# Halving by tokens at both ends of every stage, and moving the memory projections forward, in a two-layer decoder trunk

## The chip, the cores and the metric

One core of a Trainium2 chip runs the whole program. The metric is the device time of one execution in microseconds (us). TensorE (PE) does the matrix products, VectorE (DVE), ScalarE (ACT) and GpSimd (POOL) the rest; SyncE (SP) issues nearly all transfers.

## What is computed

Two layers, each of four sub-layers with the same frame: a norm before, a norm of the result, and the sum with the residual x (512 tokens, 1024 features).

```
for l in range(DEPTH):
    y = swiglu(rms_norm(x, ffn1_pre_g[l]), ...)              # 1024 -> 2816 -> 1024
    x = x + 0.5 * rms_norm(y, ffn1_post_g[l])
    y = hybrid_mixer(rms_norm(x, mix_pre_g[l]), ...)         # windowed attention heads and retention heads
    x = x + rms_norm(y, mix_post_g[l])
    y = memory_xattn(rms_norm(x, xa_pre_g[l]), rms_norm(mem, xa_mem_g[l]), wq[l], wk[l], wv[l], wo[l])
    x = x + rms_norm(y, xa_post_g[l])
    y = swiglu(rms_norm(x, ffn2_pre_g[l]), ...)
    x = x + 0.5 * rms_norm(y, ffn2_post_g[l])
```

The keys and values of the 256 memory tokens (wk, wv) depend on the memory alone, not on x.

## The kernel before

Everything is float32, in feature-major tiles: x is 8 chunks of 128 features by 512 tokens. Each operand of a product is split into a high part (rounded to the fast float32 format) and the remainder, and `mm3` (L113) adds three matmuls: high by high, high by low, low by high.

**Weights** come as units of 128 x 1024 (512 KB). `unit` (L79) fetches one over SP's queue into one of 3 raw buffers, ACT writes the high part (L85) and DVE the low part (L86) into one of 4 buffer pairs. A unit is 8 chunks k of 128 x 128, so 24 matmuls over 512 tokens.

**A stage's end.** The output projection (`out_proj` L215, or the last group of `ffn` L291) makes the 8 chunks of y; each chunk's squares are added to ssq. `postnorm` (L205) transposes ssq on PE (L162), sums it (L164), takes an inverse root by Newton steps of 11 tiny DVE operations (L129), and transposes that back to rows (L173). Then for each chunk: yn (DVE, L211), the sum into x (POOL, the first on DVE, L212), and the next stage's operand: xsh (ACT, L183) and xsl (DVE, L184).

**A stage's beginning.** The norm before a stage commutes with the product, so products start from xsh and xsl while `prenorm` (L189) squares x, sums, transposes and makes the row of scales `rstd_bc`. Results are scaled as they leave PSUM. There are 4 PSUM buffers for products (`acc`) and 4 for other work (`aux`), so 4 units can be done before `rstd_bc` is there.

**Fillers.** A stage is handed the memory work as `filler`: `mem_keys` (L369, 24 matmuls of 256 columns a unit) and `mem_values` (L381) stand ahead of the stage's own products, and `mem_split` (L356), which makes the memory's operand in 8 slots of the tag "xs", is `prep` of the stage before, six times in all. The tag "xs" has 16 slots, which also hold xsh and xsl.

**Halves already.** Before the last ffn there is no memory work left. There `out_halves` (L230) does the last two chunks of the projection by halves of 256 tokens, with `postnorm` of each half right behind it, and the first two units of the ffn run by halves too (L268).

**Order.** The text is not the order on the engines. The Tile library lists each engine's instructions ahead of time: the text's order is the priority, and what it expects to be ready later stands later. Each engine then runs its list strictly in order. So fillers and products mix matmul by matmul, and a wait that lasts longer than the list expected holds up all that stands behind it.

Of the kernel before, what the change touches and what calls it, by code (L numbers as in the profile page):

```python
# [17 lines left out]
P = 128  # L18
# [7 lines left out]
GROUPS = ((0, 8), (8, 15), (15, 22))  # L26
HALVES = (slice(0, T // 2), slice(T // 2, T))
# [20 lines left out]
def trunk(ctx: ExitStack, tc: tile.TileContext, a: dict, out: bass.AP):  # L48
# [9 lines left out]
    slots = {"b": 24, "xs": 16, "h": 16, "kv": 6}  # L58
# [34 lines left out]


    nc.sync.dma_start(small[0], a["small"][0])
    nc.sync.dma_start(x[0], a["xT"][0])
    first = {0: unit(a["ffn1_gu"][0, 0, 0], 1024)}
    for c in range(1, 4):
        nc.sync.dma_start(x[c], a["xT"][c])
    first[1] = unit(a["ffn1_gu"][0, 0, 1], 1024)  # L100
# [44 lines left out]
    def sumsq(acc_t, src, c, eng):  # L145

        if c == 0:
            n = src.shape[-1]
            acc_t = big("ssq")[:, :n]
            act.activation(acc_t, src, AF.Square)  # L150
            return acc_t
# [37 lines left out]
    def prenorm():  # L189
# [3 lines left out]
        ssq, part = None, None  # L193
        for c in range(4):
            ssq = sumsq(ssq, x[c], c, pool)
        for c in range(4, NC):
            part = sumsq(part, x[c], c - 4, dve)
        dve.tensor_tensor(ssq, ssq, part, op=ALU.add)
        cols = rms_cols(ssq, D, T)
        ps = row_bc(cols, NT)  # L200
        bc = big("rstd_bc")
        act.activation(bc, ps, AF.Copy)
        return xh, xl, cols, bc

    def postnorm(y, ssq, gains, nxt, ts_=slice(0, T)):  # L205

        w = ts_.stop - ts_.start
        ps = row_bc(rms_cols(ssq[:, ts_], D, w), w // P)
        for c in range(NC):
# [3 lines left out]
            split_x(c, nxt, ts_)  # L213

    def out_proj(src, l, oh, ol):  # L215

        y, ssq = [], None
        for c in range(NC):
            wh, wl = unit(src[l, c], 1024)
            ps = acc("ps_o")  # L220
            for k in range(NC):
                s = slice(k * P, (k + 1) * P)
                mm3(ps, wh[:, s], wl[:, s], oh[k], ol[k], k == 0, k == NC - 1)
            ssq = sumsq(ssq, ps, c, dve if c == NC - 1 else pool)
            yc = big("y")
            dve.tensor_copy(yc, ps)
            y.append(yc)
        return y, ssq

    def out_halves(src, l, oh, ol, gains, nxt):  # L230

        y, ssq, w = [], None, {}
        for c in range(NC):
            wh, wl = unit(src[l, c], 1024)
            y.append(big("y"))
            if c >= NC - 2:
                w[c] = wh, wl
                continue
            ps = acc("ps_o")
            for k in range(NC):  # L240
                s = slice(k * P, (k + 1) * P)
# [15 lines left out]
    def ffn(l, which, gains, nxt, filler=None, prep=None, halves=False):  # L257
        gu, dn = FF_UNITS[which]
        if filler:
            filler()  # L260
# [682 lines left out]
```

## Time and profile before

| | |
|---|---|
| median of 3 runs | 2509.0 us (2507.91 to 2514.05) |
| the profiled execution's own time | 2508.29 us |
| its span, first to last instruction | 2506.5 us |
| busy share PE, DVE, ACT, POOL | 97%, 56%, 36%, 10% |
| HBM traffic | 229.53 MB read, 92 GB/s over the span |
| mean granted TensorE clock | 0.995 |

Busy time of PE is modelled: a 512-column matmul is shown with 0.39 us while the next one starts 0.227 us after it, so the first 0.16 us of a wait look busy. Read the starts, not the bars.

### The profile page before, as it was taken

To read this page: it belongs to the slowest core of one execution; us is meant where nothing else is said; L and a number is where in the kernel's file an instruction comes from. 1 tells how busy PE (TensorE), PEld (TensorE's weight loads), DVE (VectorE), ACT (ScalarE), POOL (GpSimd) and SP (SyncE) were. 2 spreads that over 40 slices of the span, in tenths; PEclk is the share of its full clock that TensorE was granted. 3 is DMA by queue.
4 is the path that set the end of the run, shared out by engine and by line. 5 is a ranking of instruction groups with operands and counts; after the bars stand their busy time and mean duration, and the time that the engine had idled before them with its cause. 6 is when DMAs were issued, how large, how long until landed. Compare 5 with 4: busy or idle time off the path is not lost. (4 is left out here: it accounts for less than half of the span.)

```text
span 2506.5 us, 30782 instructions
## 1 busy us (share of the span) xinstructions
PE 2431.5 (97%) x12052; PEld 2020.5 (81%) x12052; DVE 1400.2 (56%) x2536; ACT 902.4 (36%) x1480; POOL 258.8 (10%) x218
## 2 busy tenths in 40 slices
PE   8999999999999999999999999999999998999997
PEld 6888878888877878888878888868888777888887
DVE  6434458465776484344484344584657766634454
ACT  4322243255344443222343222332553443322222
POOL 0000022001040120000120000130010402100002
PEclk9999999999999999999999999999999999999999
DMA  4333333411232233233333333324112222232321
GB/s 173 98 100 94 99 121 108 143 45 34 76 109 84 93 101 93 101 93 100 110 98 96 101 93 101 106 89 150 44 35 70 93 76 68 86 100 92 102 90 62
DMA packets 74593, 233.62 MB, mean 93 GB/s; under 512 B 8272, under 2 KB 17744, under 8 KB 74448
## 3 DMA queue, kind: packets, MB, share of 16 engines
q1 hardware_dynamic: 65232, 222.21, 27.9%
q10 hardware_dynamic: 9216, 9.44, 1.2%
q8 instruction: 95, 1.56, 0.3%
q14 instruction: 50, 0.41, 0.1%
HBM read 229.53 MB, written 2.10 MB: 92 GB/s over the span
## 5 line engine op out<-in xcount | busy, mean ns | idle before, releaser
L85 ACT ACTIVATE whi<-raw 128x1024 fp32r<-128x1024 f32 (+2 forms) x402 | 417.8, 1041 | 1097.6 <-PE ps_gu L115 324.0
L86 DVE TENSOR_TENSOR wlo<-raw,whi 128x1024 fp32r<-128x1024 f32 (+2 forms) x402 | 491.2, 1223 | 292.7 <-ACT whi L85 284.4
L114 PE MATMUL ps_gu<-xsh,whi 128*128 128x512 f32 (+1 forms) x1424 | 552.3, 389 | 13.8 <-ACT whi L85 9.3
L115 PE MATMUL ps_gu<-xsl,whi 128*128 128x512 f32 (+1 forms) x1424 | 555.0, 390 | 9.9 <-DVE xsl L184 9.7
L116 PE MATMUL ps_gu<-xsh,wlo 128*128 128x512 f32 (+1 forms) x1424 | 552.8, 388 | 0.0
L115 PEld LDWEIGHTS ps_gu<-xsl,whi 128*128 128x128 f32 x1424 | 268.6, 189 | 71.2 <-DVE xsl L184 17.7
L114 PEld LDWEIGHTS ps_gu<-xsh,whi 128*128 128x128 f32 x1424 | 269.0, 189 | 69.2 <-ACT whi L85 9.2
L116 PEld LDWEIGHTS ps_gu<-xsh,wlo 128*128 128x128 f32 x1424 | 268.8, 189 | 55.4 <-DVE wlo L86 1.8
L154 POOL TENSOR_TENSOR ssq<-ssq,sq 128x512 f32<-128x512 f32 (+1 forms) x84 | 131.4, 1564 | 1708.7 <-ACT sq L153 1705.6
L115 PE MATMUL ps_dn<-hl,whi 128*128 128x512 f32 (+1 forms) x704 | 268.5, 382 | 2.4 <-DVE hl L123 2.4
L114 PE MATMUL ps_dn<-hh,whi 128*128 128x512 f32 (+1 forms) x704 | 268.2, 381 | 0.0
L116 PE MATMUL ps_dn<-hh,wlo 128*128 128x512 f32 (+1 forms) x704 | 268.0, 381 | 0.0
L278 DVE TENSOR_TENSOR u<-ps_gu,rstd_bc 128x512 f32<-128x512 f32 x88 | 60.8, 691 | 215.4 <-PE ps_gu L116 215.3
L274 DVE TENSOR_TENSOR g<-ps_gu,rstd_bc 128x512 f32<-128x512 f32 x88 | 60.8, 691 | 183.9 <-PE ps_gu L116 179.4
L115 PEld LDWEIGHTS ps_dn<-hl,whi 128*128 128x128 f32 x704 | 132.3, 188 | 28.9 <-DVE hl L123 3.8
L114 PEld LDWEIGHTS ps_dn<-hh,whi 128*128 128x128 f32 x704 | 132.4, 188 | 26.2 <-ACT hh L122 0.5
L116 PEld LDWEIGHTS ps_dn<-hh,wlo 128*128 128x128 f32 x704 | 132.4, 188 | 25.1
L301 DVE TENSOR_TENSOR y<-ps_dn,y 128x512 f32<-128x512 f32 x56 | 38.7, 691 | 132.3 <-PE ps_dn L116 132.3
L115 PE MATMUL ps_fm<-xsl,whi 128*128 128x512 f32 x256 | 103.2, 404 | 4.0 <-DVE xsl L184 3.8
L114 PE MATMUL ps_fm<-xsh,whi 128*128 128x512 f32 x256 | 103.0, 404 | 0.0
L116 PE MATMUL ps_fm<-xsh,wlo 128*128 128x512 f32 x256 | 101.3, 396 | 0.6 <-DVE wlo L86 0.6
L612 ACT ACTIVATE p<-p,smx 128x512 f32<-128x512 f32 (+3 forms) x128 | 70.5, 552 | 87.2 <-DVE smx L610 87.0
(226 smaller groups left out, 3723.0 us busy)
## 6 DMA issues: line engine op xcount, KB each, us to landing
raw<-in_ffn_gu_dram SPq DMA_DIRECT2D x176, 512.0 KB, 3.3
raw<-in_ffn_dn_dram SPq DMA_DIRECT2D x64, 448.0 KB, 3.3
raw<-in_ffn_dn_dram SPq DMA_DIRECT2D x32, 512.0 KB, 3.5
raw<-in_win_fm_dram SPq DMA_DIRECT2D x32, 512.0 KB, 3.3
raw<-in_wk_dram SPq DMA_DIRECT2D x16, 512.0 KB, 3.5
raw<-in_cmp_w_dram SPq DMA_DIRECT2D x16, 512.0 KB, 3.7
raw<-in_wout_dram SPq DMA_DIRECT2D x16, 512.0 KB, 3.5
raw<-in_wv_dram SPq DMA_DIRECT2D x16, 512.0 KB, 3.5
```

The costliest lines, as they stand in the source:

```text
L85: act.activation(hi, raw, AF.Copy)
L86: dve.tensor_tensor(lo, raw, hi.bitcast(F32), op=ALU.subtract)
L114: pe.matmul(ps, ah, bh, start=start, stop=False)
L115: pe.matmul(ps, ah, bl, start=False, stop=False)
L116: pe.matmul(ps, al, bh, start=False, stop=stop)
L154: eng.tensor_tensor(acc_t, acc_t, sq, op=ALU.add)
L274: dve.tensor_tensor(g1, pss[0], bc, op=ALU.mult)
L278: dve.tensor_tensor(u1, pss[1], bc, op=ALU.mult)
L301: dve.tensor_tensor(y[c], ps, y[c], op=ALU.add)
L612: act.activation(pr[i], pr[i], AF.Exp, bias=m, scale=-1.0, accum_out=sums[:, i : i + 1])
```

## The change

Six things:

1. **Tail.** Every stage but the last ends with `project`: chunks 0 to 5 as before, then chunks 6 and 7 by halves of tokens from weights that `tail_unit` splits into 8 slots of "xs". Both halves' sums and rows come ahead of both `postnorm`s in the text.
2. **Lead.** `lead` starts every stage but the first with three units, fetched early, chunk by chunk: for the first 256 tokens and k = 0 to 7 all three units take their turn, then for the other 256. Three more whole units follow, two of them in `aux` buffers, before any result needs `rstd_bc`.
3. **Squares.** The squares of x are taken in each half's `postnorm` (`add_squares`), no longer in the next stage.
4. **Memory work.** Keys and values of layer 0 (16 units) stand in the first ffn's last group, ahead of chunk 5; layer 1's keys (8) in the ffn behind it and its values (8) in the third ffn. `mem_split` runs three times. No stage has a filler.
5. **Queries.** Cross-attention makes six of its eight query units in `lead`; only the last head's two are left among the heads.
6. **Buffers.** "b" has 23 slots for 24, "kv" 8 for 6, and memory chunks are fetched through 2 buffers for 3.

```diff
+FM_LEAD = (6, 7, 0, 1, 2, 3)
+N_LEAD, N_MORE, N_TAIL = 3, 3, 2
...
-    slots = {"b": 24, "xs": 16, "h": 16, "kv": 6}
+    slots = {"b": 23, "xs": 16, "h": 16, "kv": 8}
...
+    early = {}
+    def fetch(key, src):
+        early[key] = unit(src, 1024)
+    def unit_of(key, src):
+        return early.pop(key) if key in early else unit(src, 1024)
+    def tail_unit(src, n):
+        raw = raw_unit(src, n)
+        parts = []
+        for k0 in range(0, n, 512):
+            m = min(512, n - k0)
+            h_, l_ = big("dh", F32R, tag="xs")[:, :m], big("dl", F32R, tag="xs")[:, :m]
+            act.activation(h_, raw[:, k0 : k0 + m], AF.Copy)
+            dve.tensor_tensor(l_, raw[:, k0 : k0 + m], h_.bitcast(F32), op=ALU.subtract)
+            parts += [(h_[:, k : k + P], l_[:, k : k + P]) for k in range(0, m, P)]
+        return parts
...
+    squares = []
+    def add_squares(ts_):
+        if not squares:
+            squares.extend([big("ssq"), big("ssq")])
+        ssq, part = squares
+        for c in range(NC):
+            to, eng = (ssq, pool) if c < 4 else (part, dve)
+            sumsq(None if c % 4 == 0 else to[:, ts_], x[c][:, ts_], c % 4, eng, to[:, ts_])
+        dve.tensor_tensor(ssq[:, ts_], ssq[:, ts_], part[:, ts_], op=ALU.add)
+    def lead(keys, srcs, name, halves=True):
+        n = N_LEAD if halves else 2
+        units = [unit_of(key, src) for key, src in zip(keys[:n], srcs)]
+        pss = [acc(name) for _ in units]
+        for ts_ in HALVES if halves else (slice(0, T),):
+            for k in range(NC):
+                s = slice(k * P, (k + 1) * P)
+                for (wh, wl), ps in zip(units, pss):
+                    mm3(ps[:, ts_], wh[:, s], wl[:, s], xh[k][:, ts_], xl[k][:, ts_], k == 0, k == NC - 1)
+        ssq, part = squares
+        squares.clear()
+        act.activation(bc, row_bc(cols, NT), AF.Copy)
+        for i in range(n, len(keys)):
+            wh, wl = unit_of(keys[i], srcs[i])
+            ps = acc(name) if i < 4 else aux(name)
+            for k in range(NC):
+                s = slice(k * P, (k + 1) * P)
+                mm3(ps, wh[:, s], wl[:, s], xh[k], xl[k], k == 0, k == NC - 1)
+            pss.append(ps)
+        return xh, xl, pss, cols, bc
...
+        add_squares(ts_)
+    def project(src, n, oh, ol, y, ssq, gains, nxt, get=None, at=None):
+        first_y, w = y[0] is None, {}
         for c in range(NC):
+            if c == NC - N_TAIL - 1 and at:
+                at()
+            if c >= NC - N_TAIL:
+                w[c] = tail_unit(src(c), n * P)
+                if first_y:
+                    y[c] = big("y")
+                continue
+            wh, wl = unit(src(c), n * P)
             ps = acc("ps_o")
+            for k in range(n):
                 s = slice(k * P, (k + 1) * P)
+                mm3(ps, wh[:, s], wl[:, s], oh[k], ol[k], k == 0, k == n - 1)
+            if first_y:
+                y[c] = big("y")
+                dve.tensor_copy(y[c], ps)
+            else:
+                dve.tensor_tensor(y[c], ps, y[c], op=ALU.add)
+            ssq = sumsq(ssq, ps if first_y else y[c], c, pool)
+        if get:
+            get()
+        rows = []
         for ts_ in HALVES:
             for c in w:
                 ps = acc("ps_o")[:, : T // 2]
+                for k in range(n):
+                    mm3(ps, w[c][k][0], w[c][k][1], oh[k][:, ts_], ol[k][:, ts_], k == 0, k == n - 1)
+                yc = y[c][:, ts_]
+                if first_y:
+                    dve.tensor_copy(yc, ps)
+                else:
+                    dve.tensor_tensor(yc, ps, yc, op=ALU.add)
                 sq = big("sq")[:, : T // 2]
+                act.activation(sq, ps if first_y else yc, AF.Square)
                 dve.tensor_tensor(ssq[:, ts_], ssq[:, ts_], sq, op=ALU.add)
+            rows.append(row_bc(rms_cols(ssq[:, ts_], D, T // 2), NT // 2))
+        for ts_, ps in zip(HALVES, rows):
+            postnorm(y, ps, gains, nxt, ts_)
...
+    def fetch_ffn(l, which):
+        for i in range(N_LEAD):
+            f, b = divmod(i, 2)
+            fetch((which, l, f, b), a[FF_UNITS[which][0]][l, f, b])
...
+            if last:
+                project(lambda c: a[dn][l, c][:, f0 * P : f1 * P], n, hh, hl, y, None, gains, nxt, get, at)
+                return
...
-            m = bp.tile([P, MEM], F32, name="memc", tag="mc", bufs=3)
+            m = bp.tile([P, MEM], F32, name="memc", tag="mc", bufs=2)
...
-        for h in range(4):
-            if h > 0 or l == 0:
-                split_kv(h)
...
+        ready = [query(c) for c in range(n)]
+        for h in range(4):
+            if h > 0:
+                split_kv(h)
+            qs = [split(ready.pop(0) if ready else query(c), "xq") for c in range(2 * h, 2 * h + 2)]
...
-    ffn(0, "ffn1", half1[0], gcols(0, G_MIXPRE), prep=first_prep)
-    mixer(0, gcols(0, G_XAPRE), filler=keys(0, 0, 7), prep=split_mem(0))
-    xattn(0, gcols(0, G_F2PRE), filler=lambda: (mem_keys(0, 7, 8), mem_values(0, 0)), mid=values(0, 1), prep=split_mem(1))
-    ffn(0, "ffn2", half2[0], gcols(1, G_F1PRE), filler=keys(1, 0, 4), prep=split_mem(1))
-    ffn(1, "ffn1", half1[1], gcols(1, G_MIXPRE), filler=keys(1, 4, 8), prep=split_mem(1))
-    mixer(1, gcols(1, G_XAPRE), filler=values(1, 0), prep=split_mem(1))
-    xattn(1, gcols(1, G_F2PRE), filler=values(1, 1), halves=True)
-    ffn(1, "ffn2", half2[1], None, halves=True)
+    add_squares(slice(0, T))
+    ffn(0, "ffn1", half1[0], gcols(0, G_MIXPRE), get=lambda: fetch_fm(0), prep=both(mem_norm, split_mem(0)),
+        at=both(keys(0, 0, 8), values(0, 0), values(0, 1)), halves=False)
+    mixer(0, gcols(0, G_XAPRE), get=lambda: fetch_wq(0))
+    xattn(0, gcols(0, G_F2PRE), get=lambda: fetch_ffn(0, "ffn2"))
+    ffn(0, "ffn2", half2[0], gcols(1, G_F1PRE), get=lambda: fetch_ffn(1, "ffn1"), prep=split_mem(1),
+        at=both(keys(1, 0, 8)))
+    ffn(1, "ffn1", half1[1], gcols(1, G_MIXPRE), get=lambda: fetch_fm(1), prep=split_mem(1),
+        at=both(values(1, 0), values(1, 1)))
+    mixer(1, gcols(1, G_XAPRE), get=lambda: fetch_wq(1))
+    xattn(1, gcols(1, G_F2PRE), get=lambda: fetch_ffn(1, "ffn2"))
+    ffn(1, "ffn2", half2[1], None)
```

## Rows read from the trace of the kernel before

**Rows 1.** Page, part 1: busy us (share of the span) xinstructions.

```profile
PE 2431.5 (97%) x12052; PEld 2020.5 (81%) x12052; DVE 1400.2 (56%) x2536; ACT 902.4 (36%) x1480; POOL 258.8 (10%) x218
```

**Rows 2.** Busy time of PE by windows, one for each stage change: window, length, busy (xmatmuls), clock, DMA share, GB/s.

```profile
372.00:425.00 53.00, 47.53 (x294) 0.97 0.30 96
722.00:772.00 50.00, 43.70 (x194) 0.97 0.29 95
865.00:930.00 65.00, 60.88 (x309) 1.00 0.30 98
1230.00:1300.00 70.00, 64.70 (x328) 1.00 0.33 106
1620.00:1680.00 60.00, 55.16 (x238) 1.00 0.28 89
1970.00:2025.00 55.00, 49.80 (x227) 1.00 0.30 96
2085.00:2160.00 75.00, 66.30 (x370) 0.95 0.26 83
```

**Rows 3.** The same windows for tile ps_mk alone (PE, weight loads, DVE).

```profile
372.00:425.00 53.00, 22.53 (x168) 21.78 (x168) 2.65 (x7) 0.97 0.30 96
865.00:930.00 65.00, 12.13 (x96) 11.76 (x96) 1.66 (x4) 1.00 0.30 98
```

**Rows 4.** Timeline of PE: start, duration, line, tiles; 512 columns, then 256.

```profile
54.82 0.39 PE L115 MATMUL ps_gu<-xsl,whi 128*128 128x512 f32 x1
55.05 0.39 PE L116 MATMUL ps_gu<-xsh,wlo 128*128 128x512 f32 x1
...
2107.15 0.28 PE L115 MATMUL ps_o<-xol,whi 128*128 128x256 f32 x1
2107.27 0.28 PE L116 MATMUL ps_o<-xoh,wlo 128*128 128x256 f32 x1
```

**Rows 5.** Timeline of the change that already goes by halves, [idle before <-releaser].

```profile
2107.59 0.38 ACT L252 ACTIVATE sq<-ps_o 128x256 f32<-128x256 f32 x1 [2.50 <-PE ps_o L116]
...
2111.96 0.41 PE L173 MATMUL bc_ps<-cst,rs_y 128*128 128x128 f32 x2 [0.35 <-DVE rs_y L141]
...
2115.93 0.50 PE L114 MATMUL ps_gu<-xsh,whi 128*128 128x256 f32 x2 [1.43 <-ACT xsh L183]
...
2126.40 0.43 PE L173 MATMUL bc_ps<-cst,rs_y 128*128 128x128 f32 x2 [2.78 <-DVE rs_y L141]
...
2129.65 0.58 PE L114 MATMUL ps_gu<-xsh,whi 128*128 128x256 f32 x1 [2.82 <-ACT xsh L183]
```

**Rows 6.** Timeline of DVE: first yn and last xsl of that change's second half.

```profile
2126.87 0.87 DVE L211 SCALAR_TENSOR_TENSOR yn<-y,small,bc_ps 128x256 f32<-128x256 f32 x2 [0.53 <-PE bc_ps L173]
...
2135.69 0.49 DVE L184 SCALAR_TENSOR_TENSOR xsl<-x,small,xsh 128x256 fp32r<-128x256 f32 x1 [0.29 <-ACT xsh L183]
```

**Rows 7.** Groups by line and form: xcount | busy us, mean ns | idle before.

```profile
L184 DVE SCALAR_TENSOR_TENSOR xsl<-x,small,xsh 128x512 fp32r<-128x512 f32 x56 | 63.6, 1136 | 6.6 <-PE ps_mv L116 3.4 <-ACT xsh L183 3.1
L184 DVE SCALAR_TENSOR_TENSOR xsl<-x,small,xsh 128x256 fp32r<-128x256 f32 x16 | 8.5, 549 | 1.8 <-ACT xsh L183 1.8
L154 DVE TENSOR_TENSOR ssq<-ssq,sq 128x256 f32<-128x256 f32 x2 | 0.9, 426 | 1.1 <-ACT sq L153 1.1
L212 POOL TENSOR_TENSOR x<-x,yn 128x256 f32<-128x256 f32 x14 | 11.5, 849 | 18.6 <-DVE yn L211 18.6
```

**Rows 8.** Windows: ps_tm at the end of the first mixer's heads, and all engines (PE, loads, DVE, ACT, POOL) in the second cross-attention.

```profile
640.00:656.00 16.00, 15.47 (x67) 12.50 (x67) 2.44 (x4) 1.00 0.44 142
...
2016.00:2083.00 67.00, 66.47 (x341) 52.83 (x339) 41.34 (x82) 30.29 (x67) 0.00 (x0) 1.00 0.13 43
```

**Rows 9.** Windows, all engines, behind the longest wait of the kernel.

```profile
2124.00:2136.00 12.00, 6.78 (x31) 6.34 (x32) 9.71 (x30) 4.65 (x10) 5.75 (x7) 0.72 0.14 44
```

**Rows 10.** Page part 6 (KB each, us to landing) and DVE's weight split of part 5.

```profile
raw<-in_wk_dram SPq DMA_DIRECT2D x16, 512.0 KB, 3.5
L86 DVE TENSOR_TENSOR wlo<-raw,whi 128x1024 fp32r<-128x1024 f32 (+2 forms) x402 | 491.2, 1223 | 292.7 <-ACT whi L85 284.4
```

More of the change, by code (lines that the diff above doesn't have):

```diff
@@ L265, in ffn @@
             for f in range(f0, f1):
-                w = [first.pop(b) if b in first else unit(a[gu][l, f, b], 1024) for b in range(2)]
-                pss = [acc("ps_gu") for _ in range(2)]
-                for ts_ in HALVES if halves and f == 0 else (slice(0, T),):
-                    for (wh, wl), ps in zip(w, pss):
-                        for k in range(NC):
-                            s = slice(k * P, (k + 1) * P)
-                            mm3(ps[:, ts_], wh[:, s], wl[:, s], xh[k][:, ts_], xl[k][:, ts_], k == 0, k == NC - 1)
+                pss = []
+                for b in range(2):
+                    if lead_ps:
+                        pss.append(lead_ps.pop(0))
+                        continue
+                    wh, wl = unit(a[gu][l, f, b], 1024)
+                    ps = acc("ps_gu")
+                    for k in range(NC):
+                        s = slice(k * P, (k + 1) * P)
+                        mm3(ps, wh[:, s], wl[:, s], xh[k], xl[k], k == 0, k == NC - 1)
+                    pss.append(ps)
                 g1 = big("g1")
@@ L301, in ffn @@
                     dve.tensor_tensor(y[c], ps, y[c], op=ALU.add)
-                if last:
-                    ssq = sumsq(ssq, y[c], c, dve if c == NC - 1 else pool)
-        postnorm(y, ssq, gains, nxt)
     def down_halves(src, f0, n, hh, hl, y, gains):
@@ L358, in mem_split @@
         for c in range(NC):
[L359 removed]
+            m = bp.tile([P, MEM], F32, name="memc", tag="mc", bufs=2)
             nc.scalar.dma_start(m, a["memT"][c])
@@ L395, in mem_values, with mixer @@
             kv["v", l, m, half] = t
-    def mixer(l, nxt, filler=None, prep=None):
+    def mixer(l, nxt, get=None, prep=None, at=None):
         sm = small[l]
-        if filler:
-            filler()
-        xh, xl, cols, bc = prenorm()
+        xh, xl, lead_ps, cols, bc = lead([("fm", l, j) for j in FM_LEAD], [a["win_fm"][l, j] for j in FM_LEAD], "ps_fm")
+        lead_ps = dict(zip(FM_LEAD, lead_ps))
         def fm(j):
+            if j in lead_ps:
+                return lead_ps.pop(j)
             wh, wl = unit(a["win_fm"][l, j], 1024)
@@ L758, in split_kv, with query @@
                     vv[m, h // 2] = pair(kv["v", l, m, h // 2], "xv")
[L760 to L770 removed]
+        split_kv(0)
+        n = N_LEAD + N_MORE
+        xh, xl, lead_ps, cols, bc = lead([("wq", l, c) for c in range(n)], [a["wq"][l, c] for c in range(n)], "ps_xq")
+        oh, ol = [], []
+        def query(c):
+            if lead_ps:
+                ps = lead_ps.pop(0)
+            else:
                 wh, wl = unit(a["wq"][l, c], 1024)
```

102 lines of the change are left out of this document (25 added, 77 removed).

## The prediction

> **What bounds the kernel now.** The page first: PE is busy 97% of the span, no other engine over 56%, PE's weight loads aside [rows 1]. The kernel is its matmuls, so a change can only cut their number, their spacing, or PE's waits. Nothing here cuts the number. Spacing comes next, from the timeline: in a stream of 512-column matmuls one starts 0.227 us after another, of 256 columns 0.120 [rows 4]. Two halves cost 0.240, so halving adds 0.013 us a matmul and 0.040 a chunk of three.
>
> Then the waits, by windows around the seven stage changes [rows 2]. They hold 428 us and, less a dozen that began earlier, 1948 matmuls. Of these 600 have 256 columns (384 are memory keys, of which 168 and 96 stand in [rows 3]; the window at 722 has 24 and that at 1230 again 96; 192 are halves in the last window, 24 are scores), 126 are narrow at 0.11 (16 transposes a window), and 1222 have 512. At their spacings that is 72 + 14 + 277 = 363 us; **65 us are lost**, about 9 a change, although 90 us of memory work (384 key matmuls, 46 us, and 192 value matmuls of 512 columns, 44) ran in and around six of them. Part of it is the clock: behind a wait from 2123 to 2130 [rows 5] the granted clock averages 0.72 over 12 us [rows 9], that is, part of the time at 1.2 instead of 2.4 GHz, 3.4 us lost. The windows at 372 and 722 show 0.97, 1.6 us each.
>
> The last window matters most: it has no memory work and already goes by halves, and it loses 14 us, the most of all. There the second half's scales reached PE after a wait of 2.78 us and its first operand after 2.82 more [rows 5], because the text put the first half's `postnorm` ahead of the second half's sums.
>
> **The change part by part.** The sum is made against the profiled execution, 2508.3 us, which lies 0.7 under the median.
>
> *Halves, on PE's path.* A lead has 3 units x 8 chunks x 0.040 = 0.96 us more, a tail 2 x 8 x 0.040 = 0.64 (7 chunks in an ffn: 0.56). Seven leads, four tails of 8 and three of 7 make 6.7 + 2.6 + 1.7 = 11.0. The last change pays 1.3 of this already: **+9.7 us**.
>
> The Trainium skill, "TensorE: Matmul & The Clock Gate", section "Back-to-back issue gap", gives 518 cycles for 512 columns and 262 for 256, so two halves would cost 6 cycles or 2.5 ns more, and the whole term 2 us. Here rows 4 show 13 ns; the row decides.
>
> *What is lost at a change afterwards.* Count from the end E of the first half's tail. The first yn can start 4.8 us later: from the square at 2107.59 to the end of the row transposes at 2112.37 [rows 5]. PE meanwhile has the second half's tail, 48 x 0.120 = 5.8 us. The next stage's first matmul needs yn, sum and xsh besides, some 1.5 us, plus 0.4 in an ffn, where y is summed before it is squared: PE waits about 1.0. In the trace it was 1.43 [rows 5].
>
> DVE sets the rest. One half of `postnorm` with DVE nearly to itself took 9.3 us, from the first yn at 2126.87 to the end of the last xsl at 2136.18 [rows 6]. Two are 18.6. Between them, by the order of the text, stand the second half's last sums and its Newton steps (at most 3.6: the first half's chain of 4.8 less ACT's square of 0.38 and two lots of transposes of 0.41) and the first half's squares, 4 x 0.43 = 1.7 [rows 7]. Without overlap the last xsl ends at E + 4.8 + 18.6 + 5.3 = E + 28.7 and PE's last leading chunk, 9 x 0.12 = 1.1, at 29.8. PE's own work from E is 5.8 + 2 x 8 x 1.1 + 0.9 of transposes = 24.0. So 5.8 us are lost if nothing overlaps; if the 1.4 us in which DVE waits inside each half are filled by the other's work, 3.0. I take 4.6, and 1.5 for the three places where PE's list holds transposes that come late: **6.1 us a change**, between 3.0 and, as in the last window less its clock, 10.5. The three whole units behind the lead (72 x 0.227 = 16.3 us) cover the remaining squares and `rstd_bc`, some 8 to 10 us.
>
> Seven changes: 43 us for 65. No wait of this sum is as long as the two of rows 5 together, so I expect no stretch like that of rows 9 and no loss by the clock.
>
> *Memory work.* It moves, and its 90 us of matmuls stay. In the last groups PE does a key unit in 24 x 0.120 = 2.9 us. Its cover is the supply: three raw buffers, each taken for 3.5 us of landing [rows 10] and some 2.3 for the two splits (DVE's is 1.22 [rows 10]), give a unit every 1.9 us. Were only one transfer in flight, 16 units would each be 0.6 late: +10 us at most. I take 0. Three `mem_split`s fewer take 24 transfers off ACT's queue and some 24 operations off ACT and DVE, which are not the bound: 0. Two buffers for three make the remaining ones slower while ACT's list holds weight splits behind them: +1, between 0 and 4.
>
> *Fetches.* The three early units are queued on SP behind the tail's raw units, and their splits stand before E on ACT and DVE, where rows 1 show room: 0. On POOL the squares double in number at half the width, 0.
>
> *Fill taken from later work.* Queries and mixer units done before `rstd_bc` no longer fill gaps afterwards: six instead of four, 11 us a stage. In the first mixer 15.5 us of filling work were left when the heads had ended [rows 8], so 4 remain. In the second cross-attention DVE was busy 41 us of 67 [rows 8]; with 11 us fewer on PE it still fits. One slot of "b" fewer may stretch the heads. Together +1, between 0 and 8.
>
> Sum: 2508.3 - 65 + 43 + 9.7 + 2 = **2498 us**. From the bounds (3.0 and no extras; 8.5 and 4 of extras) this case spans 2474 to 2517; its middle is 2485 to 2509.
>
> **The rivals.**
>
> *All of it overlaps, 2474.* DVE's waits are filled and no transposes come late, 3.0 a change: 2508 - 65 + 21 + 10. For it: DVE works 9.7 us of 12 even in the stretch of rows 9, so little of it is idle to begin with. Against: that is the engine's order in hindsight.
>
> *As much is lost as before, 2511.* The cover of the memory work is gone and every change loses 8, which with the halves is what there was. For it: fillers of 11 us and more (96 x 0.120 [rows 3]) did cover the first chain. The library may also reorder so that the halves run into each other and the change does less than it says.
>
> *Slower, 2528.* One mechanism: DVE's list. The second half's sums and Newton steps now stand ahead of the first half's `postnorm`. DVE runs strictly in order, so if they come later than listed, both halves wait behind them and PE behind both. The only halved change in the trace lost 14 us, 10.5 without its clock; seven at 10.5 are 73.5, and 2508 - 65 + 73.5 + 11.7 is 2528. It decides where the second half's first xsl comes over 5 us behind the end of PE's leading chunks of the first half.
>
> *Heads run dry, 2514.* If a head's softmax isn't overlapped with the next head's scores, the fill of 11 us is missed: +8 in each cross-attention. Against: with six queries ready, scores of several heads can run.
>
> *DVE and POOL block each other, 2539.* Each xsl has two inputs in SBUF and runs while POOL sums x. At 512 columns it took 1.136 us in the mean, at 256 only 0.549 [rows 7]. Were each of 16 held up by half a POOL sum (0.849 [rows 7]), a change would lose 6 us more, 42 in all. The Trainium skill, "SBUF — State Buffer", section "Who interferes with whom", says that a VectorE instruction with two SBUF inputs and a GpSimd instruction reading SBUF exclude each other for a whole instruction. By that rule this rival would hold; a mean of 0.549 for twice the work of a half says that it seldom decides.
>
> **How the numbers follow.** A difference under 0.3% (7.5 us) can't be told from none. The forecast has 0.50 (0.38 of it faster, 0.12 the same), full overlap 0.16 (faster), as much lost as before 0.10 (0.08 same, 0.02 slower), DVE's list 0.16 (slower), dry heads 0.05 (0.03 same, 0.02 slower), blocking 0.03 (slower). Faster 0.54, same 0.23, slower 0.23. The range goes from full overlap to most of the case of DVE's list: 2474 to 2522.
>
> **What would show it.** In the changed profile each stage change should show PE waiting about 1 us behind the tail, short waits chunk by chunk in the lead, and no window with a clock under 0.95. The products ps_mk and ps_mv should stand unbroken ahead of the last down chunks at 2.9 us a unit. The forecast is wrong if transposes of rms_ps or bc_ps again show waits of 2 us or more on PE, if ps_mk or ps_mv wait on transfers, or if PE idles among the heads.

## The result and the profile after

After the change a run takes 2563.6 us (median of 4, 2561.7 to 2564.4), against 2508.5 (4 runs, 2505.3 to 2514.1) on the same chip: ratio 1.022, 95% interval 1.0207 to 1.0233. That is **55 us slower**, outside the range and on the other side of the forecast. The profiled run took 2562.9 us, with a span of 2561.2. Part 1 of the page, for [rows 1]:

```profile
PE 2466.5 (96%) x12778; PEld 2082.9 (81%) x12778; DVE 1422.0 (56%) x2764; ACT 919.5 (36%) x1586; POOL 243.3 (9%) x275
```

The seven changes of stage in the kernel after, as windows: stretch and length, busy time of PE, PEld, DVE, ACT, POOL (xinstructions), granted clock, DMA share, GB/s. They answer to [rows 2].

```profile
418.00:465.00 47.00, 40.43 (x253) 35.54 (x253) 38.03 (x99) 16.83 (x38) 18.48 (x28) 0.96 0.08 25
755.00:808.00 53.00, 44.91 (x274) 39.12 (x273) 40.00 (x99) 21.08 (x44) 16.82 (x20) 0.97 0.15 50
885.00:940.00 55.00, 48.19 (x314) 42.96 (x313) 43.52 (x106) 24.18 (x49) 18.57 (x21) 0.97 0.15 49
1285.00:1340.00 55.00, 47.99 (x300) 41.77 (x300) 43.57 (x105) 23.73 (x49) 18.59 (x21) 0.97 0.16 55
1685.00:1735.00 50.00, 43.22 (x273) 38.23 (x273) 39.45 (x102) 16.83 (x38) 18.41 (x28) 0.97 0.10 32
2030.00:2082.00 52.00, 43.81 (x267) 38.06 (x266) 39.52 (x98) 21.03 (x44) 16.81 (x20) 0.97 0.16 51
2160.00:2215.00 55.00, 48.15 (x309) 42.55 (x308) 43.84 (x106) 23.43 (x48) 18.60 (x21) 0.97 0.14 49
```

All seven look alike now: PE idles 6.6 to 8.2 us in each and DVE is busy three quarters to four fifths of it. Four of the seven had an unbroken clock in [rows 2]; none has now. What PE waits for in the second window, by the view of waits (engine, line, what ended the wait, us in total, times, longest):

```profile
PE bc_ps L196 <- DVE rs_y L164: 2.3, 3, 1.7
PE ps_xq L137 <- ACT xsh L206: 1.8, 2, 1.4
PE rms_ps L185 <- DVE ssq L222: 1.5, 1, 1.5
PE rms_ps L185 <- DVE ssq L299: 1.5, 1, 1.5
PE ps_xq L138 <- DVE xsl L207: 0.8, 3, 0.3
```

5.3 us of it stand at transposes; over the seven changes it is 3.2 to 5.3. For all runs below I took what the prediction calls lost: from one matmul's start to the next, less the spacing of its form [rows 4]; 0.110 us for transposes and narrow products, 0.130 and 0.174 for 280 and 384 columns. Summed over the trace, in us ("ahead": the last 20 us before a stage's first product; "behind": the 50 us after it, or up to the compression or the scores; both mixers and both cross-attentions together):

```
                        before  e12_mem  e3_whole   after
products at their spacing 2372.3  2372.3   2371.1   2381.7
lost, changes, ahead         8.7    62.5     65.4     19.8
lost, changes, behind       57.3    50.2     22.3     64.9
lost, compression            0.2     1.9     10.4     10.7
lost, retention             10.5    10.5     18.4     18.4
lost, attention heads        6.2     7.1     15.0     14.0
lost, elsewhere             33.3    36.1     40.9     35.5
```

Columns one and four are the result: 9.4 us more products, 18.7 more lost at the changes, 26.2 more in compression, retention and heads. Columns two and three are runs that make the change in parts. Against e12_mem, which moves the memory work (and the buffers with it) and nothing else, the changed kernel loses 28.0 us less at the changes and pays 9.4 in products and 23.6 in compression, retention and heads: what the halves, the leads and the early queries win, they give back.

### The profile page after: what moved, and what is told of

Read it like the earlier page. It is cut to its first block, busy times and chain, and to the rows that moved or that the text cites. A ratio compares the mean times of both kernels' runs of the same rounds, so it can differ in the third digit from the quotient of the medians.

```text
span 2561.2 us, 32626 instructions
## 1 busy us (share of the span) xinstructions
PE 2466.5 (96%) x12778; PEld 2082.9 (81%) x12778; DVE 1422.0 (56%) x2764; ACT 919.5 (36%) x1586; POOL 243.3 (9%) x275
## 4 chain that ended last, share of the span: by engine, by line
PE 83%; DVE 8%; ACT 3%; POOL 2%; DMA 2%; issue 2%; ACTq 0%; POOLq 0%; SPq 0%; DVEq 0%
PE ps_gu L137 12%; PE ps_gu L138 12%; PE ps_gu L139 11%; PE ps_dn L137 5%; PE ps_dn L139 5%; PE ps_dn L138 5%; PE ps_o L138 3%; PE ps_o L139 3%; PE ps_o L137 3%; PE ps_po L698 3%; POOL x L257 2%; PE ps_fm L137 2%; PE ps_fm L139 2%; PE ps_fm L138 2%; PE ps_tm L138 1%
## 5 line engine op out<-in xcount | busy, mean ns | idle before, releaser
L87 ACT ACTIVATE whi<-raw 128x1024 fp32r<-128x1024 f32 (+3 forms) x388 | 402.8, 1042 | 984.9 <-PE ps_gu L138 336.0
L88 DVE TENSOR_TENSOR wlo<-raw,whi 128x1024 fp32r<-128x1024 f32 (+3 forms) x388 | 469.2, 1210 | 250.8 <-ACT whi L87 244.2
L177 POOL TENSOR_TENSOR ssq<-ssq,sq 128x256 f32<-128x256 f32 (+1 forms) x99 | 113.3, 1144 | 1759.2 <-ACT sq L176 1707.8
L137 PE MATMUL ps_dn<-hh,whi 128*128 128x512 f32 (+1 forms) x536 | 202.7, 378 | 0.0
L138 PE MATMUL ps_dn<-hl,whi 128*128 128x512 f32 (+1 forms) x536 | 202.6, 378 | 0.0
L139 PE MATMUL ps_dn<-hh,wlo 128*128 128x512 f32 (+1 forms) x536 | 202.6, 378 | 0.0
L137 PE MATMUL ps_fm<-xsh,whi 128*128 128x512 f32 (+1 forms) x304 | 110.4, 376 | 6.8 <-ACT xsh L206 3.6
L138 PE MATMUL ps_fm<-xsl,whi 128*128 128x512 f32 (+1 forms) x304 | 114.7, 379 | 2.2 <-DVE xsl L207 1.9
L139 PEld LDWEIGHTS ps_dn<-hh,wlo 128*128 128x128 f32 x536 | 100.8, 188 | 18.7
L139 PE MATMUL ps_fm<-xsh,wlo 128*128 128x512 f32 (+1 forms) x304 | 111.5, 369 | 0.0
L257 POOL TENSOR_TENSOR x<-x,yn 128x256 f32<-128x256 f32 x98 | 84.7, 873 | 123.6 <-DVE yn L256 96.1
```

Source lines behind the costliest of these rows:

```text
L87: act.activation(hi, raw, AF.Copy)
L88: dve.tensor_tensor(lo, raw, hi.bitcast(F32), op=ALU.subtract)
L137: pe.matmul(ps, ah, bh, start=start, stop=False)
L138: pe.matmul(ps, ah, bl, start=False, stop=False)
L139: pe.matmul(ps, al, bh, start=False, stop=stop)
L177: eng.tensor_tensor(acc_t, acc_t, sq, op=ALU.add)
```

## The experiments

The changed kernel is 2563.6 us in what follows, the kernel before 2507.4 to 2508.5 by the runs beside each. Ratios are to the kernel before.

**Memory work forward, and nothing else (e12_mem).** In the kernel before; `at` is called ahead of the last three down chunks, all six fillers go, and the buffers are those of the change.

```
-    mixer(0, gcols(0, G_XAPRE), filler=keys(0, 0, 7), prep=split_mem(0))
+    mixer(0, gcols(0, G_XAPRE))
...
+                if last and at and c == NC - 3:
+                    at()
...
+    ffn(0, "ffn1", ..., prep=first_prep, at=both(keys(0, 0, 8), values(0, 0, 1)))
+    ffn(0, "ffn2", ..., prep=split_mem(1), at=keys(1, 0, 8))
+    ffn(1, "ffn1", ..., prep=split_mem(1), at=values(1, 0, 1))
```

> The kernel before with one thing of the change: the memory work goes ahead of the last down chunks of three feed-forwards, and six changes of stage stand without it. Theory, it was cover: the first chain (9.3 us from the last chunk to the first split, as in the run with whole tails) and the single units fed chunk by chunk lie open, some 12 us a change more: 2508 + 72, about 2580 us. Rival, the work hid little, as the prediction had it that the changes lost 9 us in spite of it: 2508 to 2525 us.

2560.2 us, 1.0212 (1.0197 to 1.0228): **53 of the 55 us come with this step alone**. In the table it is one entry, ahead of the next stage's first product, 8.7 to 62.5. The waits of PE at the change behind the first mixer in this run, from 760 us to 790:

```profile
PE bc_ps L173 <- DVE rs_y L141: 3.2, 1, 3.2
PE ps_xq L114 <- ACT xsh L183: 2.9, 1, 2.9
PE rms_ps L162 <- DVE ssq L154: 2.8, 1, 2.8
PE ps_xq L115 <- DVE xsl L184: 1.6, 1, 1.6
```

The first three are one chain, last chunk to first split: some 9 us. Here is a window of 22 us that begins less than 1 us ahead of the projection's last product, in this run and then in the kernel before:

```profile
760.00:782.00 22.00, 13.11 (x45) 9.49 (x43) 18.08 (x31) 8.27 (x13) 11.38 (x7) 0.69 0.10 36
```

```profile
721.00:743.00 22.00, 20.75 (x102) 16.11 (x100) 18.78 (x33) 13.68 (x20) 9.87 (x7) 1.00 0.27 86
```

Before, PE was busy for all but 1.3 us, first with ps_mk and ps_mv, and the chain ran underneath. Without them it is idle for 8.9 us and the granted clock of the window is 0.69. The size was 53 for the expected 72, because the loss behind the first product did not grow (57.3 to 50.2).

**Whole tails and leads (e3_whole), and halves where cover remains (e13_halves).** First the changed kernel, in `lead` and, with the widths to match, in `project`:

```
-        for ts_ in HALVES if halves else (slice(0, T),):
+        for ts_ in (slice(0, T),):
...
-        for ts_ in HALVES:
+        for ts_ in (slice(0, T),):
...
-        for ts_, ps in zip(HALVES, rows):
+        for ts_, ps in zip((slice(0, T),), rows):
```

> The changed kernel with tails and leads of all 512 tokens, all else as it stands. Theory, halving is worth its overlap: without it PE waits from the last chunk to the first split, some 10 us, is then fed chunk by chunk, and the clock falls, some 18 us a change for 12 now; less 9.7 us of halving: 2563.6 + 42 - 9.7, about 2596 us. Rival, halving brings nothing, because DVE's list is as long and the second half's scales come late: the loss stays at 12 to 13 a change and the 9.7 us are saved, 2552 to 2562 us.

2557.3 us, 1.0199 (1.0183 to 1.0214): 6 us under the changed kernel by the medians, which is less than the 0.3% that the prediction asks for, and no slower; the rival held. (The profiled run is the slowest of the four, so the third column shows only 1.3 us of the 6.) Third column: halves take 45.6 us from "ahead" and put 42.6 into "behind", and the products grow by 10.6. The reason is a length on DVE. The change behind the first mixer from the tail's last product to the last split, timeline (start, duration, engine, line, tiles, [idle <-releaser]), first with halves (the kernel after; the rows at 775 and 777 us are the end of PE's leading chunks of the first half and the second half's first split), then whole:

```profile
760.59 0.28 PE L138 MATMUL ps_o<-ol,dh 128*128 128x256 f32 x1
760.71 0.28 PE L139 MATMUL ps_o<-oh,dl 128*128 128x256 f32 x1
...
761.37 0.47 DVE L256 SCALAR_TENSOR_TENSOR yn<-y,small,bc_ps 128x256 f32<-128x256 f32 x1
...
775.30 0.28 PE L139 MATMUL ps_xq<-xsh,wlo 128*128 128x256 f32 x1
...
777.37 0.95 DVE L207 SCALAR_TENSOR_TENSOR xsl<-x,small,xsh 128x256 fp32r<-128x256 f32 x1
...
786.15 0.48 DVE L207 SCALAR_TENSOR_TENSOR xsl<-x,small,xsh 128x256 fp32r<-128x256 f32 x1 [1.17 <-ACT xsh L206]
```

```profile
765.32 0.39 PE L139 MATMUL ps_o<-oh,dl 128*128 128x512 f32 x1
...
772.82 1.41 DVE L256 SCALAR_TENSOR_TENSOR yn<-y,small,bc_ps 128x512 f32<-128x512 f32 x2 [1.21 <-PE bc_ps L196]
...
786.17 3.49 DVE L207 SCALAR_TENSOR_TENSOR xsl<-x,small,xsh 128x512 fp32r<-128x512 f32 x2
```

With halves the first yn stands 0.7 us behind the last product instead of 7.5, yet the last split ends 25.9 behind it instead of 24.3: 53 DVE operations for 33. In all seven changes the last split comes 25.9 to 26.0 us behind with halves and 24.3 to 24.9 whole. PE can't end a lead before DVE's last split, so the early start only turned one long wait into many. Next the kernel before, both mixers, the first cross-attention and the lead behind it:

```
-        y, ssq = out_proj(a["wout"], l, oh, ol)
-        postnorm(y, ssq, gcols(l, G_MIXPOST), nxt)
+        out_halves(a["wout"], l, oh, ol, gcols(l, G_MIXPOST), nxt)
+    xattn(0, ..., prep=split_mem(1), halves=True)
+    ffn(0, "ffn2", ..., prep=split_mem(1), halves=True)
```

> The kernel before with its own half tails at three more changes (behind both mixers and the first cross-attention, and the lead behind the latter), the memory work staying where it is. Theory, the memory work already hides the chain from the last chunk to the first split, so there is nothing for half tails to shorten, and they lengthen DVE's list and PE's products (0.6 to 1.3 us a change) and take two of four weight buffers from the memory units: 2507 + 5 to 15, about 2517 us. Rival, half tails and cover add up, and the waits of 7 to 11 us of these changes fall by the 6.5 us by which halving cut the first chain elsewhere: 2507 - 15, about 2492 us.

2513.9 us, 1.0024 (1.0015 to 1.0034), as the theory had it, a little less: where the chain is hidden, halves have nothing to shorten.

**Memory work back at the changes, halves kept (e4_cover).** Six fillers ahead of the leads, kept chunks in the ring of split weights, nothing fetched early:

```
-                w[c] = tail_unit(src(c), n * P)
+                wh, wl = unit(src(c), n * P)
+                w[c] = [(wh[:, k * P : (k + 1) * P], wl[:, k * P : (k + 1) * P]) for k in range(n)]
...
-    mixer(0, gcols(0, G_XAPRE), get=lambda: fetch_wq(0))
+    mixer(0, gcols(0, G_XAPRE), filler=keys(0, 0, 7), prep=split_mem(0))
...
```

> The changed kernel with halves as they are, but the memory work back between a stage's tail and the next lead as before (eight or fewer units at six changes), and nothing fetched early. Theory, what the change gave up is cover: DVE's work between two stages takes longer than PE's whatever the halves do, and 11 to 23 us of memory products on PE hide it; six changes lose 4 to 5 us instead of 12: about 2520 us. Rival, the loss is in PE's order (transposes that come late) and stays whatever stands there, and the units' splits lengthen DVE's list: 2560 to 2575 us.

2571.7 us, 1.0259 (1.0242 to 1.0276). The theory's number fell and the rival's range holds the result, but the run doesn't show the rival's cause, because it brings waits of its own. PE's longest wait behind the first cross-attention:

```profile
919.00 0.55 PE L137 MATMUL ps_gu<-xsh,whi 128*128 128x256 f32 x1 [7.16 <-DVE mk L445]
```

The lead's products wait until DVE has taken a memory product out of PSUM (`mk`), which stands late on DVE's list; at the second cross-attention PE waits 5.9 us for a wlo (up to 2046 us), where tails, memory units and the lead share the ring. The fill lost in compression and heads stays lost (10.6 and 16.3). e12_mem and e13_halves answer what it mixed.

**DVE's list (e6_newton, e14_newton, e5_late).** In `newton`, the first in the changed kernel and the second in the kernel before:

```
-        for _ in range(3):
+        for _ in range(1):
```

> The changed kernel with one Newton iteration instead of three in every inverse root (it leaves out two of three iterations). Theory, DVE's list: six operations of 0.15 to 0.25 us fewer on the way to the first half's scales and six among the first half's postnorm, 2.4 us a change, and 0.3 to 1 in each of some ten other chains: 2563.6 - 17 to -25, about 2543 us. Rival, the operations stand in gaps in which DVE waits for GpSimd's sums anyway: only the 1.2 us ahead of the scales count, 2555 us.

> The kernel before with one Newton iteration instead of three (two of three left out), the edit that took 23 us from the changed kernel. Theory, in the kernel before the memory work hides these chains at six changes, and only the last change, the heads' ends and the two retentions show them: 2507 - 6, about 2501 us. Rival, the chains lie open in both kernels alike: 2507 - 20, about 2487 us.

With two of the three iterations left out: 2540.9 us, 1.0126 (1.0107 to 1.0144), 23 less than the change; in the kernel before 2501.0, 0.9972 (0.9961 to 0.9984), 6.6 less. Both expectations were met: some 16 us of Newton steps lie open only since the change. DVE's timeline in the kernel after, first half's postnorm, and one of GpSimd's sums of x beside it:

```profile
425.93 0.84 DVE L207 SCALAR_TENSOR_TENSOR xsl<-x,small,xsh 128x256 fp32r<-128x256 f32 x1
426.69 0.15 DVE L189 TENSOR_SCALAR rms_v<-rms_s 128x2 f32<-128x2 f32 x1
426.76 0.47 DVE L256 SCALAR_TENSOR_TENSOR yn<-y,hg,bc_ps 128x256 f32<-128x256 f32 x1
427.15 0.15 DVE L155 TENSOR_SCALAR rs_i<-rms_v 128x2 int32<-128x2 int32 x1
427.22 0.47 DVE L207 SCALAR_TENSOR_TENSOR xsl<-x,small,xsh 128x256 fp32r<-128x256 f32 x1
427.62 0.69 DVE L157 TENSOR_SCALAR rs_y<-rs_i 128x2 int32<-128x2 int32 x1
428.23 0.47 DVE L256 SCALAR_TENSOR_TENSOR yn<-y,hg,bc_ps 128x256 f32<-128x256 f32 x1
428.62 0.15 DVE L160 TENSOR_TENSOR rs_t<-rs_y 128x2 f32<-128x2 f32 x1
428.86 0.93 DVE L207 SCALAR_TENSOR_TENSOR xsl<-x,small,xsh 128x256 fp32r<-128x256 f32 x1
...
427.31 0.98 POOL L257 TENSOR_TENSOR x<-x,yn 128x256 f32<-128x256 f32 x1 [0.82 <-DVE rs_i L155]
```

The second half's scales (rms_v to rs_t) are threaded through the first half's chunks, one step between any two operations. An xsl takes 0.47 or 0.93 us, and one step of 128x2 takes 0.69: it starts inside GpSimd's sum and ends with it.

In e5_late the squares go from the end of `postnorm` to the end of `project`:

```
             split_x(c, nxt, ts_)
-        add_squares(ts_)
...
             postnorm(y, ps, gains, nxt, ts_)
+        add_squares(slice(0, T))
```

> The changed kernel with the squares of x summed once, after both halves of the postnorm and at full width, instead of half by half. Theory, DVE's list is the length of a stage change: between the halves DVE now has four sums of 0.52 us and one of 0.42 less, 2.5 us a change, which PE stops waiting for: 2563.6 - 17, about 2546 us. Rival, the last sums and the chain of rstd_bc behind them come later and PE waits there instead: 2560 to 2568 us.

2577.6 us, 1.0274 (1.0254 to 1.0293): 14 us the other way, further than the rival. The waits at the transposes in the second change, for the lines of the kernel after with 1.5 (longest 1.5) and 2.3 (longest 1.7):

```profile
PE rms_ps L185 <- DVE ssq L222: 3.0, 1, 3.0
PE bc_ps L196 <- DVE rs_y L164: 3.7, 3, 3.1
```

Operations saved between the halves came back at the end of the same list, with the chain of rstd_bc behind them.

**VectorE and GpSimd (e7_xdve, e15_sums).** In `postnorm`, the first in the changed kernel and the second in the kernel before:

```
-            (dve if c == 0 else pool).tensor_tensor(x[c][:, ts_], x[c][:, ts_], t, op=ALU.add)
+            dve.tensor_tensor(x[c][:, ts_], x[c][:, ts_], t, op=ALU.add)
```

> The changed kernel with all sums of x on VectorE instead of seven of eight on GpSimd. Theory, VectorE alone is the bound: 14 operations of 0.42 us more in each change, 5.9 us, which PE waits for: 2563.6 + 41, about 2604 us. Rival, VectorE and GpSimd hold each other up: a split of 0.63 us falls to 0.47 and the Newton steps to 0.15, and a chunk's chain loses a GpSimd sum of 0.87: at most 1.5 us a change either way, 2553 to 2574 us.

2560.4 us, 1.0203 (1.0186 to 1.0220), 3 us under the changed kernel, too little to tell from none: 98 more DVE operations cost nothing. Groups by form, the kernel after, then this run:

```profile
L207 DVE SCALAR_TENSOR_TENSOR xsl<-x,small,xsh 128x256 fp32r<-128x256 f32 x112 | 70.9, 633 | 22.7 <-ACT xsh L206 20.6
L160 DVE TENSOR_TENSOR rs_t<-rs_y 128x2 f32<-128x2 f32 x51 | 11.7, 229 | 0.8
```

```profile
L207 DVE SCALAR_TENSOR_TENSOR xsl<-x,small,xsh 128x256 fp32r<-128x256 f32 x112 | 57.6, 525 | 4.6 <-ACT xsh L206 4.6
L160 DVE TENSOR_TENSOR rs_t<-rs_y 128x2 f32<-128x2 f32 x51 | 8.2, 160 | 0.8
```

Splits and these Newton steps shrink by 108 and 69 ns once GpSimd no longer adds x beside them. The Trainium skill, "SBUF — State Buffer", section "Who interferes with whom", has it that a VectorE instruction with two SBUF inputs contends with a GpSimd instruction that reads SBUF, and that this is an exclusive lock; these rows agree. A step with one input (rs_y from rs_i, 128x2) shrinks as well, from 386 to 169 ns, which that sentence does not cover.

> The kernel before with all sums of x on VectorE instead of seven of eight on GpSimd. Theory, the two hold each other up: a chunk's chain of sum and split takes 0.68 + 0.95 us instead of 1.65 + 1.14, and of the waits of 1.0 to 1.6 us, one per chunk, that PE has behind the memory work, 2 to 4 us a change go: 2507.5 - 20, about 2487 us. Rival, VectorE's list is only longer, by 7 sums of 0.68 us a change that lie between the splits: 2507.5 + 10 to 25, about 2525 us.

2512.9 us, 1.0026 (1.0017 to 1.0035): 5.5 slower, so the theory fell there. At 512 columns the splits shrink from 1136 [rows 7] to 859 ns, 2.2 us a change, but seven sums of 706 ns add 4.9. So the two hold each other up at both widths; what differs is whether taking the sums off GpSimd pays. Why it costs nothing with halves and 5.5 us at full width no run shows: by the count of operations alone VectorE's list grew in both.

**More units beside each other (e8_lead4, e10_bclate, e9_two, e16_sums_two).** The first two are the changed kernel:

```
-N_LEAD, N_MORE, N_TAIL = 3, 3, 2
+N_LEAD, N_MORE, N_TAIL = 4, 2, 2
```

> The changed kernel with four units instead of three in each halved lead, and two whole units behind it instead of three. Theory, in a change DVE needs some 32 us whatever PE does, and the loss is that time less the PE work that may run in it: a fourth unit puts 5.8 us more of it there, of which some 5 count, and the two units left (10.9 us) still cover the chain of rstd_bc: 2563.6 - 7 x 5 + 2, about 2530 us. Rival, PE waits for transposes that come late in its own order, not for DVE's chunks: 2555 to 2565 us.

2588.3 us, 1.0316 (1.0295 to 1.0336): 25 slower, not 33 faster. The timeline of PE behind a lead:

```profile
795.21 0.60 PE L185 MATMUL rms_ps<-cst,ssq 128*128 128x128 f32 x4
803.71 1.08 PE L196 MATMUL bc_ps<-cst,rs_y 128*128 128x128 f32 x4 [7.90 <-DVE rs_y L164]
```

The waits for chunks are gone (0.4 us left at the first), and the chain of rstd_bc, 7.9 us, lies open: bc_ps stands in PE's order ahead of the units meant to cover it.

In e10_bclate `lead` has, besides:

```
-        bc = big("rstd_bc")
-        act.activation(bc, row_bc(cols, NT), AF.Copy)
         for i in range(n, len(keys)):
...
             pss.append(ps)
+        bc = big("rstd_bc")
+        act.activation(bc, row_bc(cols, NT), AF.Copy)
```

> The run of four units a lead, with the row transposes of rstd_bc behind the two whole units instead of ahead of them. There PE waited 8.1 us for them at each change, and no longer for DVE's chunks. Theory, with something to do in that time the fourth unit pays after all: 2588.3 - 7 x 5.5, about 2550 us, 13 under the changed kernel. Rival, the two units cannot start, because their weights wait for the lead's buffers: 2575 to 2590 us.

2573.1 us, 1.0262 (1.0248 to 1.0276), between theory and rival. The changes fall to 76.4 us lost (84.7 in the changed kernel), as the theory wants, but the compression loses 22.8 for 10.7. PE's longest wait there, in each mixer:

```profile
PE ps_hid L522 <- DVE cf L511: 4.4, 1, 4.4
```

`cf` is made from two of the lead's results, which can't be scaled before `rstd_bc`: the late row holds up the next stage's work.

e9_two is the kernel before; in the mixers and cross-attentions the first two units are joined in the same way:

```
-                    for (wh, wl), ps in zip(w, pss):
-                        for k in range(NC):
+                    ks = [(k, b) for k in range(NC) for b in range(2)] if f == 0 else [(k, b) for b in range(2) for k in range(NC)]
+                    for k, b in ks:
```

> The kernel before with one thing of the change: the first two units of a stage go chunk by chunk, side by side, instead of one behind the other; memory work, tails and widths stay. Theory, behind the memory work PE is fed by DVE one chunk after another, 24 waits of 1.0 to 1.9 us in seven changes, and two units give it twice the work in each of them: 2 to 3 us less a change, 2508 - 15, about 2493 us. Rival, the last chunk comes when it came and PE's waits only gather elsewhere: 2505 to 2511 us.

2506.8 us, 0.9997 (0.9988 to 1.0006): nothing. The last split of each change comes when it came, within 0.1 us counted from the last product of the stage before, as the rival said.

e16_sums_two has the edits of e9_two and e15_sums together.

> The same with the first two units of a stage going chunk by chunk. Theory, DVE's last chunk comes earlier, but it still sets the end of the lead, so that the order of PE's products before it changes little: within 3 us of the run with the sums alone. Rival, chunks that come faster than one unit's 0.68 us of products leave PE behind, and two units side by side lose what one after the other would not: 3 to 8 us faster or slower than it.

2513.2 us, 1.0023 (1.0013 to 1.0034), within 0.3 us of the sums alone. So no part of the change that I tried alone beats the kernel before.

**Fill and lists inside the stages (e1_fm, e2_dec, e11_tail).** All three are the changed kernel. In e1_fm three retention queries, evicted as soon as `rstd_bc` is there, replace the three mixer queries:

```
-FM_LEAD = (6, 7, 0, 1, 2, 3)
+FM_LEAD = (6, 7, 0, 8, 9, 10)
...
+        qr = [fm_plain(8 + h, "qr", "h") for h in range(RH - 1)]
```

> Against the changed kernel's 2563.6 us. Theory, the compression has lost its company: three query projections now stand in the lead, the compression's eight units carry 1.8 us of matmuls each and run one behind another, and PE waits for their transfers; the stretches behind both leads lost 5.1 and 5.4 us for 0.1 and 0.2 before. With three retention projections in the lead instead they go back to that: 2553 us, and no wait of ps_fm or ps_hid on a transfer there. Rival, the fill is missed wherever it is taken from: what is won there is lost behind the heads, 2560 to 2566.

2565.7 us, 1.0233 (1.0217 to 1.0248): no gain. The compression as windows (columns as above), in the kernel after, then in this run:

```profile
465.00:513.00 48.00, 46.36 (x301) 42.45 (x299) 19.64 (x34) 10.41 (x19) 1.49 (x8) 0.93 0.48 158
```

```profile
466.00:520.00 54.00, 54.00 (x327) 48.14 (x326) 22.96 (x40) 7.51 (x11) 1.48 (x8) 1.00 0.40 129
```

The compression's 10.7 us are gone, to 0.2, as in the kernel before; the retention rises from 18.4 to 32.3. A product taken as cover at one end is missed at the other.

In e2_dec GpSimd issues the decay transfer of the retention heads:

```
-            nc.scalar.dma_start(dec, a["decay"][h])
+            nc.gpsimd.dma_start(dec, a["decay"][h])
```

> Against the changed kernel's 2563.6 us. Theory, ACT's list: the decay transfer of a retention head is issued by ACT behind the first split of the projection's kept weights, which waits for its raw transfer, and PE waits 2.5 to 2.7 us for the products in each mixer. Issued by GpSimd the transfer waits for nothing: both waits go, 2558.5 us. Rival, the score stretch is bound by DVE or by its buffers, and the wait turns up behind another instruction: 2562 to 2565.

2564.3 us, 1.0229 (1.0213 to 1.0244): the rival. ACT's timeline in the kernel after, with its queue:

```profile
689.58 1.05 ACT L87 ACTIVATE whi<-raw 128x1024 fp32r<-128x1024 f32 x1
696.25 0.63 ACT L112 ACTIVATE dh<-raw 128x512 fp32r<-128x512 f32 x1 [5.62 <-DMA raw<-in_wout_dram]
696.26 0.34 ACTq L759 DMA_DIRECT2D dec<-in_decay_dram  x1
```

A kept chunk's split waits 5.6 us for its weights, and the decay transfer behind it goes out only then. With the transfer on GpSimd, PE waited 3.2 us at the same place, for `ra` on DVE, where the other half of that split (`dl`) stands ahead of the score products.

In e11_tail, for the mixers alone (`ring`), with two units of `wq` fetched instead of three:

```
-                w[c] = tail_unit(src(c), n * P)
+                if ring:
+                    wh, wl = unit(src(c), n * P)
+                    w[c] = [(wh[:, k * P : (k + 1) * P], wl[:, k * P : (k + 1) * P]) for k in range(n)]
+                else:
+                    w[c] = tail_unit(src(c), n * P)
```

> The changed kernel, but in both mixers the last two chunks are kept in the ring of split weights as before, not in buffers of their own, and two units of the next stage are fetched instead of three. Theory, in the retention PE waits because the splits of the kept weights stand on ACT's and DVE's lists ahead of the score work while their transfer is on its way: the score stretch goes back from 8.3 us lost to 3.8 in each mixer: 2563.6 - 9, about 2555 us. Rival, the third unit of the lead comes late instead: 2560 to 2567 us.

2559.1 us, 1.0209 (1.0195 to 1.0223), 4.5 us under the changed kernel and again less than 0.3%. The retention is back to 10.5, as the theory said. Of these 7.9 us 4.3 are lost again behind the first products; of those 2.6 lie behind the two mixers, where the third unit is fetched late (its wlo, 1.76 us on DVE at 776.4, stands among the splits of xsl), and the rest at changes that the edit doesn't touch.

The heads of the cross-attention have no edit of their own. Their waits in the kernel after, 808 to 885 us (none in the kernel before), then in e12_mem, which leaves the queries among the heads, 790 to 890 us:

```profile
PE ps_xt L873 <- DVE xp L868: 1.8, 2, 1.3
PE ps_xo L137 <- ACT xpTh L145: 0.6, 1, 0.6
```

```profile
PE bc_ps L173 <- DVE rs_y L141: 0.2, 1, 0.2
```

So the heads' loss comes with what e12_mem lacks and e3_whole already has (15.0 in the table): the early queries are the likeliest part of it, but no run has them alone.

## Why the prediction was wrong

**The step that failed is "what is lost at a change afterwards: 6.1 us".** It measured 12.1 (84.7 in seven). Three of its parts were too small (they overlap and don't add up, since PE waits for DVE's last split whatever came late before it):

- *DVE.* The working put the last split at E + 28.7, 22.9 behind the second tail's last product; it came 25.9 behind. The stretched operations of the timeline above are in that; the rows of the one halved change, with 16 splits at 0.549, did not show them so long.
- *Overlap.* It took 4.6 between 5.8 (none) and 3.0. The second half's Newton steps did run among the first half's chunks, but nothing was won by it: the last split came 3 us behind the sum without any overlap.
- *PE's order and the clock.* 1.5 us stood for late transposes. They cost 3.2 to 5.3, of which 1.3 to 3.2 stand behind the lead, where no split hides them. "No loss by the clock" did not hold: 0.96 or 0.97 in all seven windows and 0.93 in the compression, though no stretch like that of rows 9. By the prediction's own measure (1.6 us for a window at 0.97) that is some 11 us at the seven changes, as an estimate and at most, for PE waits for DVE again soon after.

**"Memory work: 0" was right where it went and wrong about what it left.** Tile ps_mk in the second feed-forward's last group, against [rows 3] (PE, weight loads, DVE):

```profile
1231.00:1285.00 54.00, 23.20 (x192) 23.17 (x192) 3.39 (x8) 1.00 0.55 170
```

192 products in 23.2 us, PE busy all through, no wait for a transfer. But the 65 us of the kernel before were read as what a change costs in spite of the memory work, as if that cover could be taken off and only the new chain counted. The cover hid 53.8 us more (e12_mem). The rival "as much lost as before" named this, with a chance of 0.10, and priced it at 8 us a change; it is what the runs show, at 12.

**"Fill taken from later work: +1, 0 to 8" measured 26**: compression 10.5, retention 7.9, heads 7.8. The prediction looked at what was left at the heads' end and at DVE's busy share, not at the compression, whose products of 64 columns lived off the queries between them. Heads running dry was a rival at 8 us a stage; it cost 3.9. The retention's share is no fill: kept weights put a waiting split ahead of other work on two in-order lists (e11_tail); the step "Fetches" asked only whether DVE and ACT had room for these splits, and took 0.

**Right:** the halves' 9.7 us (spacing 0.12 in the tail lines above; 9.4 more of products, counted from those spacings); and slower memory splits at +1, where PE waited 1.5 us for memg in the first feed-forward. DVE's list, given 0.16 at 2528, is right in that the list's length sets the change (e6_newton), but not in the way described: the second half's first split starts 2.0 us behind the end of PE's leading chunks (777.37 against 775.30 and one spacing of 0.12, in the lines of e3_whole), not over 5. The two blocking each other, given 0.03 at 42 us, is seen at both widths (e7_xdve, e15_sums), but ending it brought 3 us with halves and cost 5.5 at full width.

**The signs.** Of the three signs of being wrong only the last came, PE idling among the heads. No transpose made PE wait 2 us (the longest wait was 1.9) and ps_mk and ps_mv waited on no transfer: a threshold on the single wait let pass five waits of 0.2 to 1.7 us in one change.

Sum by what was measured: -66.0 + 84.7 + 9.4 + 26.2 + 2.2 elsewhere = +56.5 from the first product on; that one starts 1.7 us earlier (at 7.6 instead of 9.3), and the span grew by 54.7. What stays open: an order in which halves and memory work stand at a change together with their weights in time; the one run that tried it (e4_cover) had them late.

## What to carry to other kernels

Work that PE does while a chain runs elsewhere is worth the length of that chain, not its own: before moving it, take the chain's length from a place where it lies open, and count that as the price. Cutting a step in halves starts the engine behind it sooner but ends it no sooner when another engine's list sets the last piece, so compare the time to the last piece, not to the first. Products taken as cover from a later place must be missed nowhere there: look for the short-product stretches that live off them.

## What the runs showed of the hardware that was not expected

Behind the open chain the granted clock of a 22 us window was 0.69 in the mean, that is, part of the time at 1.2 instead of 2.4 GHz, where the same place with memory products ran at 1.00. VectorE operations of 128x2 elements took 0.15 us, or 0.69 where a GpSimd sum ran beside them (427.31 to 428.29 us in the lines of e6_newton), so a dozen tiny steps are not tiny there.
